# Masked softmax on one core: narrow loads into staging buffers, with a copy on VectorE

## The chip, the core and the metric

The kernel runs on one core of a Trainium2 chip. The metric is device time in microseconds, from one execution of the program. Before the change three runs gave 156.01, 156.16 and 156.28 us, median 156.16.

A core has engines that each follow an instruction queue of their own: VectorE (DVE in the profile), ScalarE (ACT), GpSimd (POOL), TensorE (PE) and SyncE (SP), which here only issues transfers. Sixteen DMA engines move data between HBM (the large memory, where inputs and outputs lie) and SBUF (the on-chip memory, 128 partitions wide). Engines wait for one another and for transfers by semaphores: counters that an instruction or a landed transfer raises and that another waits for.

## What is computed

The input `x` has 16 batches of 8 heads of 256 x 256 float32; `lengths` has one number per batch, between 128 and 255. Each row of 256 is softmaxed over its first `length` columns, and the other columns of the result are zero:

```python
for b in range(batch):
    length = lengths[b]
    masked = x[b, :, :, :length].copy()
    masked = masked - np.max(masked, axis=-1, keepdims=True)
    exp_masked = np.exp(masked)
    result[b, :, :, :length] = exp_masked / np.sum(exp_masked, axis=-1, keepdims=True)
```

The lengths of this draw are 188, 233, 229, 243 for the first four batches and 195, 252, 165, 210, 222, 180, 209, 157, 159, 199, 214, 248 for the other twelve.

## The kernel before

**Tiling.** A batch is 2,048 rows of 256 floats. It is one tile: 128 partitions with 16 rows (`nt`) of 1 KB each, 2.1 MB. A partition's 16 rows are neighbours in HBM. `xt` holds eight such tiles (`slots`), and batch b uses slot b % 8. Everything is done in place: loaded, masked, exponentiated, divided and stored from the same slot.

**Loads.** SP loads batches 0 to 3 whole, at the start (lines 128 to 132, batch 0 as two halves). The other twelve are issued by POOL in a loop (line 177). For each, POOL reads the batch's length into a register (line 180, the load itself is line 120) and walks a binary tree of branches, `pick`, that ends at one of twelve loads: the smallest of the widths 160, 168, ..., 240, 256 that is no less than the length. Only so many columns of each row are fetched, into a tile whose rows keep their distance of 1 KB (line 151). Widths here are 200, 256, 168, 216, 224, 184, 216, 160, 160, 200, 216, 256. From the third of these loads on, POOL first waits for the load two before it (`s_sw`, line 182) and, from batch 8 on, for the store of the batch eight before it, whose slot it takes (`s_st`, line 183; the semaphore starts with 64 counted, so that the first pair passes). Columns that a narrow load leaves out hold zeros from a fill (line 173) or what an earlier batch left there; the mask covers both.

**VectorE.** For each batch: `mask` (line 230) reads the length into a register, waits for the load, and in one instruction, `clip` (line 221), takes the minimum of x and a huge falling ramp `down` + `len_s`, which leaves the first `length` columns and makes the others hugely negative. Only the columns from 128 on are treated, since no length here is under 128; that is 128 x 2048 elements. `clip` raises `s_min` by two. After ScalarE's exponentials, `divide` (line 242) is done for each half of the rows: a reciprocal of the row sums (line 245) and a multiply (line 248).

The order on VectorE is fixed. For batch 0 and from batch 4 on it is divide(b, first half), mask(b+1), divide(b, second half); for batches 1 to 3 it is mask(b+1), divide(b, first half), divide(b, second half). So the mask of batch 4 stands ahead of both divides of batch 3.

**ScalarE** loops over 32 half tiles (line 321): it waits for `s_min`, then does eight exponentials of 256 elements with row sums (line 326). The slot is found in registers, as the loop's counter modulo 16.

**Stores.** SP issues one to three transfers per batch (`parts`, line 51; line 141), each when `divide` has raised `s_out`, and before the first of a batch it waits for the stores of the batch two before it (line 140). At the end SP waits for the last two batches' stores.

No maximum is subtracted. After the last batch VectorE tests that all row sums are within bounds, and an exact second pass stands ready if they aren't (from line 272); it isn't entered with this input.

Of the kernel before, what the change touches and what calls it, by code (L numbers as in the profile page):

```python
# [9 lines left out]
F32 = mybir.dt.float32  # L10
# [7 lines left out]
POOL = mybir.EngineType.Pool  # L18
# [3 lines left out]
def kernel(  # L22
# [6 lines left out]
    nc = tc.nc  # L29
    P = nc.NUM_PARTITIONS  # L30

    batch, heads, seq_q, seq_k = x.shape
    rows = heads * seq_q
    assert rows % P == 0
    nt = rows // P
# [3 lines left out]
    x_f = x.rearrange("b h q k -> b (h q) k").rearrange("b (p t) k -> b p t k", p=P)  # L39
    out_f = out.rearrange("b h q k -> b (h q) k").rearrange("b (p t) k -> b p t k", p=P)  # L40

    slots = 8
    ahead = 4
    assert slots - ahead == 4 and batch % slots == 0

    widths = list(range(160, 248, 8))
    low = widths[0]
    mid = seq_k // 2
# [15 lines left out]
    pool = ctx.enter_context(tc.tile_pool(name="all", bufs=1))  # L64
    psum = ctx.enter_context(tc.tile_pool(name="psum", bufs=1, space=bass.MemoryType.PSUM))
    xt = pool.tile([P, slots, nt, seq_k], F32, name="xt")
    word64 = pool.tile([1, batch], mybir.dt.int64, name="word64")
    word = word64.bitcast(I32)
    len_b = pool.tile([1, batch], BF16, name="len_b")
# [21 lines left out]
    sem = lambda n: ctx.enter_context(nc.semaphore(n))  # L91
    s_st = [sem("s_st0"), sem("s_st1")]
    with tc.tile_critical(no_gpsimd_drain=True):  # L93
# [3 lines left out]
        s_lenf = sem("s_lenf")  # L97
        s_ld = [sem(f"s_ld{k}") for k in range(ahead + 1)]

        s_sw = [sem("s_sw0"), sem("s_sw1")]  # L100

        s_iota = sem("s_iota")
        s_fill = sem("s_fill")
        s_v = sem("s_v")
        s_min = sem("s_min")
# [12 lines left out]
        def length(engine, at):  # L118

            return nc.values_load(  # L120
                at,
                engines=[engine],
                skip_runtime_bounds_check_because="compared with constants, never an address",
            )
# [3 lines left out]
        for h in range(2):  # L128
            s = slice(h * half, (h + 1) * half)
# [5 lines left out]
        for b in range(batch):  # L135
            s_b = s_st[b % 2]
            for s in parts(b):
                nc.sync.wait_ge(s_out, 2 * b + (s.stop - 1) // half + 1)
                if b >= 2 and s.start == 0:
                    nc.sync.wait_ge(s_b, 64 * (b // 2 + 1))  # L140
                nc.sync.dma_start(
                    out=out_f[b, :, s, :], in_=xt[:, b % slots, s, :]
# [1 line left out]

        def pick(v, n, slot, par, ws):

            if len(ws) == 1:
                w = ws[0]  # L150
                nc.gpsimd.dma_start(  # L151
                    out=xt[:, slot, :, :w], in_=x_n[:, n, :, :w]
                ).then_inc(s_sw[par], 16)
                return
            m = (len(ws) - 1) // 2
            with nc.gpsimd.If(v <= ws[m]):  # L156
                pick(v, n, slot, par, ws[: m + 1])
            with nc.gpsimd.Else():
                pick(v, n, slot, par, ws[m + 1 :])

        x_n = x_f.rearrange("b p t c -> p b t c")
        x_g = x_f.rearrange("b p t c -> p b (t c)")
# [6 lines left out]
        for par in range(2):  # L169
            nc.gpsimd.memset(seed[:, par : par + 1], 0.0).then_inc(s_st[par], 64)  # L170
        nc.gpsimd.wait_ge(s_v, 2)
        for b in range(ahead, slots):
            nc.gpsimd.memset(xt[:, b, :, low:], 0.0).then_inc(s_fill, 1)  # L173
        nc.gpsimd.wait_ge(s_word, 16)
        nc.gpsimd.wait_ge(s_fill, slots - ahead)
        nc.gpsimd.wait_ge(s_ld[ahead - 1], 16)
        with nc.Fori(0, (batch - ahead) // 2, 1, engines=[POOL]) as q:
            for par in range(2):
                n = 2 * q + (ahead + par)
                v_len = length(POOL, word[0:1, bass.ds(2 * n, 1)])  # L180
                with nc.gpsimd.If(q >= 1):  # L181
                    nc.gpsimd.wait_ge(s_sw[par], 16 * q)
                    nc.gpsimd.wait_ge(s_st[par], 64 * q)
                pick(v_len, bass.ds(n, 1), bass.ds(n % slots, 1), par, widths + [seq_k])


        nc.tensor.wait_ge(s_ones, 2)
# [6 lines left out]
        v = 0  # L194

        def step(ins):
# [8 lines left out]
                out=down, in0=iota_i, scalar1=0.5, scalar2=-big, op0=ALU.add, op1=ALU.mult  # L205
# [7 lines left out]
                out=len_s, in0=len_f, scalar1=big, scalar2=None, op0=ALU.mult  # L213
# [1 line left out]
        )  # L215
        nc.vector.wait_ge(s_v, v)

        def clip(b, s, lo, hi):

            t = xt[:, b % slots, s, lo:hi]  # L220
            return nc.vector.scalar_tensor_tensor(  # L221
                out=t,
                in0=down[:, None, lo:hi].to_broadcast([P, s.stop - s.start, hi - lo]),
                scalar=len_s[:, b : b + 1],
                in1=t,
                op0=ALU.add,
                op1=ALU.min,
            )

        def mask(b, s):  # L230
            v_len = length(DVE, word[0:1, 2 * b : 2 * b + 1])
            if b == 0:
                nc.vector.wait_ge(s_ld[s.start // half], 16)
            elif b < ahead:
                nc.vector.wait_ge(s_ld[b + 1], 16)
            else:
                nc.vector.wait_ge(s_sw[b % 2], 16 * ((b - ahead) // 2 + 1))
            with nc.vector.If(v_len < mid):
                clip(b, s, 0, mid)
            clip(b, s, mid, seq_k).then_inc(s_min, (s.stop - s.start) // half)  # L240

        def divide(b, h):
            s = slice(h * half, (h + 1) * half)
            nc.vector.wait_ge(s_exp, 2 * b + h + 1)
            step(nc.vector.reciprocal(out=inv_sum[:, b, s], in_=row_sum[:, b, s]))  # L245
            nc.vector.wait_ge(s_v, v)
            t = xt[:, b % slots, s, :]
            nc.vector.tensor_tensor(  # L248
                out=t,
                in0=t,  # L250
                in1=inv_sum[:, b, s, None].to_broadcast([P, half, seq_k]),
                op=ALU.mult,
            ).then_inc(s_out, 1)

        mask(0, slice(0, half))
        mask(0, slice(half, nt))
        for b in range(batch):


            first = b == 0 or b >= ahead  # L260
            if first:
                divide(b, 0)
            if b + 1 < batch:
                mask(b + 1, slice(0, nt))
            if not first:
                divide(b, 0)
            divide(b, 1)
# [8 lines left out]
        for k, (edge, op) in enumerate(((sum_high, ALU.is_gt), (sum_low, ALU.is_lt))):  # L276
            nc.vector.tensor_scalar(  # L277
                out=bad[:, k : k + 1],
# [13 lines left out]
        with nc.vector.Else():  # L292
            with nc.Fori(0, batch, 1, engines=[DVE]) as i:
                nc.vector.wait_ge(g_ld, 16 * i + 16)
                nc.vector.scalar_tensor_tensor(
                    out=g_t,
                    in0=down[:, None, :].to_broadcast([P, nt, seq_k]),
                    scalar=len_s[:, bass.ds(i, 1)],
                    in1=g_t,
# [5 lines left out]
                    out=neg_max, in_=g_t, op=ALU.max, axis=AX, negate=True  # L305
# [5 lines left out]
                    out=g_t,  # L311
                    in0=g_t,
                    in1=inv_g[:, :, None].to_broadcast([P, nt, seq_k]),
# [7 lines left out]
        with nc.Fori(0, 2 * batch, 1, engines=[ACT]) as i:  # L321
            nc.scalar.wait_ge(s_min, i + 1)
            at = bass.ds(i % (2 * slots), 1)
            for j in range(half):
                e = x_h[:, at, j, :]
                ins = nc.scalar.activation(  # L326
                    out=e, in_=e, func=EXP, accum_out=sum_h[:, bass.ds(i, 1), j]
# [5 lines left out]
        with nc.scalar.If(a_redo >= 1):  # L333
            for par in range(2):
                nc.scalar.wait_ge(s_st[par], 64 * (batch // 2 + 1))
            with nc.Fori(0, batch, 1, engines=[ACT]) as i:
                nc.scalar.dma_start(out=g_t, in_=x_g[:, bass.ds(i, 1)]).then_inc(g_ld, 16)
                nc.scalar.wait_ge(g_v, 3 * i + 2)
                for t in range(nt):
                    ins = nc.scalar.activation(  # L340
                        out=g_t[:, t],
                        in_=g_t[:, t],
# [43 lines left out]
```

## Time and profile before

| | before |
|---|---|
| median of three runs | 156.16 us |
| the profiled execution | 156.34 us |
| its span, first to last instruction | 154.7 us |
| DMA | 62.09 MB, 401 GB/s over the span |
| VectorE busy | 116.6 us (75%) |
| ScalarE busy | 105.2 us (68%) |
| POOL busy | 19.0 us (12%) |
| last multiply ends | 147.11 us |

The span lies inside the execution; the rest of 156.34 is outside what the instructions cover. A row of the profile names the source line (L221), the engine, the operation, the tiles (written <- read) and their shapes; behind a bar stand the busy time in us and the mean of one in ns, then the engine's idle time ahead of these instructions and what ended it. Engine names with a q, as POOLq, are the engine's instruction queue: register work, branches and the issuing of transfers. In the slice rows the span is cut into 40 equal parts, and a digit is the busy share in tenths. A queue row of the DMA part gives packets, MB, and the packets' time as a share of 16 engines' span; q1 carries SP's transfers, q0 those of POOL.

### The profile page before, as it was taken

The numbers are of one execution on the slowest core, as the hardware profiler recorded it, in microseconds if no ns is written. First come the engines' busy times: TensorE is split into PE (matmuls) and PEld (weight loads), VectorE is DVE, ScalarE is ACT, GpSimd is POOL, SyncE is SP. The second block draws the span as 40 slices with busy tenths as digits, with TensorE's granted clock in tenths as the row PEclk, the third lists the DMA queues.
The fourth block names the chain that finished last, engine by engine and source line by source line (L and its number), as shares of the span: only waits on it lengthen the run. The fifth ranks groups of instructions, "written<-read, shape, count | busy, mean of one in ns | idle before, by whom it ended". The sixth has DMA issues, their size and how long they took to land.

```text
span 154.7 us, 1341 instructions
## 1 busy us (share of the span) xinstructions
PE 0.3 (0%) x2; PEld 0.2 (0%) x2; DVE 116.6 (75%) x89; ACT 105.2 (68%) x514; POOL 19.0 (12%) x26
## 2 busy tenths in 40 slices
PE   0000000000000000000000000000000000000000
PEld 0000000000000000000000000000000000000000
DVE  1349999953999696979879696969669619696820
ACT  3097799992692959688695959595964914959300
POOL 4910031000220200202020020202001000000000
DMA  3999999999999999999999999999999999999991
GB/s 114 430 447 419 441 373 420 403 407 447 406 403 391 410 410 417 412 416 412 404 422 409 415 412 409 421 414 412 415 424 415 416 437 432 422 447 424 424 426 76
DMA packets 9989, 62.09 MB, mean 401 GB/s; under 512 B 850, under 2 KB 946, under 8 KB 6274
## 3 DMA queue, kind: packets, MB, share of 16 engines
q1 hardware_dynamic: 5904, 41.95, 65.7%
q0 software_dynamic: 4080, 20.12, 32.1%
q14 instruction: 3, 0.02, 0.0%
q10 hardware_dynamic: 2, 0.00, 0.0%
HBM read 28.51 MB, written 33.55 MB: 401 GB/s over the span
## 4 chain that ended last, share of the span: by engine, by line
DMA 77%; issue 7%; DVE 4%; ACT 3%; POOLq 3%; SPq 1%; ACTq 0%; POOL 0%; PE 0%; DVEq 0%
DMA xt<-in_x_dram 77%; ACT xt L326 3%; DVE xt L221 2%; DVE xt L248 1%; POOLq L120 1%; POOLq L156 1%; POOLq L151 1%; SPq L130 1%; DVE ends L274 0%; ACTq L326 0%; POOL xt L151 0%; SPq L132 0%; POOLq L181 0%; DVE bad L277 0%; DVE inv_sum L245 0%
## 5 line engine op out<-in xcount | busy, mean ns | idle before, releaser
L326 ACT ACTIVATE xt<-xt x256 | 102.4, 402 | 37.7 <-DVE xt L221 37.7
L248 DVE TENSOR_TENSOR xt<-xt,inv_sum 128x2048 f32<-128x2048 f32 x32 | 73.3, 2291 | 1.1
L326 ACT ACTIVATION_READ_ACCUMULATOR xt<-xt x256 | 48.0, 188 | 0.0
L221 DVE SCALAR_TENSOR_TENSOR xt<-down,len_s,xt 128x2048 f32<-128x2048 f32 (+1 forms) x17 | 37.8, 2221 | 13.6 <-DMA xt<-in_x_dram 13.5
L151 POOL DMA_DIRECT2D xt<-in_x_dram x12 | 12.8, 1064 | 96.0 <-DMA out_dram<-xt 54.2
L245 DVE RECIPROCAL inv_sum<-row_sum 128x8 f32<-128x8 f32 x32 | 6.3, 198 | 14.4 <-ACT xt L326 14.4
L173 POOL MEMSET xt<- 128x1536 f32 x4 | 5.3, 1391 | 1.1 <-DVE len_s L212 1.1
L318 ACT ACT_TABLE_LOAD x1 | 1.3, 1283 | 1.6 <-SPq L93 1.6
L204 DVE TENSOR_SCALAR down<-iota_i 128x256 f32<-128x256 int32 x1 | 0.3, 301 | 1.6 <-POOL iota_i L164 1.6
L274 DVE TENSOR_REDUCE ends<-row_sum 128x1 f32<-128x256 f32 x2 | 0.7, 411 | 0.0
L191 PE MATMUL count<-bad,ones_c 128*1 128x2 bf16 x1 | 0.2, 164 | 145.3 <-DVE bad L277 145.3
L209 DVE CAST len_b<-word 1x16 bf16<-1x16 int32 x1 | 0.2, 164 | 0.4 <-DMA word<-in_lengths_dram 0.4
L212 DVE TENSOR_SCALAR len_s<-len_f 128x16 f32<-128x16 f32 x1 | 0.2, 173 | 0.3 <-PE len_f L189 0.3
L164 POOL IOTA iota_i<- 128x256 int32 x1 | 0.3, 331 | 0.6 <-SPq L93 0.6
L285 DVE TENSOR_REDUCE redo<-count 1x1 f32<-1x2 f32 x1 | 0.1, 148 | 0.3 <-PE count L191 0.3
L191 PEld LDWEIGHTS count<-bad,ones_c 128*1 128x1 bf16 x1 | 0.1, 79 | 145.4 <-DVE bad L277 145.4
L170 POOL MEMSET seed<- 1x1 f32 x2 | 0.2, 226 | 0.0
L277 DVE TENSOR_SCALAR bad<-ends 128x1 bf16<-128x1 f32 x2 | 0.2, 152 | 0.0
L318 ACT ACTIVATE warm<-const-float32-0.0 128x1 f32<-128x1 f32 x1 | 0.2, 204 | 0.0
L167 POOL MEMSET ones<- 1x128 bf16 x1 | 0.2, 196 | 0.0
L189 PE MATMUL len_f<-len_b,ones 1*128 1x16 bf16 x1 | 0.2, 165 | 2.6 <-DVE len_b L209 2.6
L370 POOL MEMSET const-float32-0.0<- 128x1 f32 x1 | 0.1, 98 | 0.3 <-issue 0.3
(6 smaller groups left out, 0.5 us busy)
## 6 DMA issues: line engine op xcount, KB each, us to landing
out_dram<-xt SPq DMA_DIRECT2D x19, 1024.0 KB
out_dram<-xt SPq DMA_DIRECT2D x14, 512.0 KB
xt<-in_x_dram SPq DMA_DIRECT2D x3, 2048.0 KB, 16.0
out_dram<-xt SPq DMA_DIRECT2D x3, 2048.0 KB
xt<-in_x_dram POOLq DMA_DIRECT2D x3, 1728.0 KB, 16.9
xt<-in_x_dram POOLq DMA_DIRECT2D x2, 2048.0 KB, 18.5
xt<-in_x_dram POOLq DMA_DIRECT2D x2, 1600.0 KB, 17.1
xt<-in_x_dram POOLq DMA_DIRECT2D x2, 1280.0 KB, 15.1
```

Of the source, the lines that this page charges most:

```text
L120: return nc.values_load(at, engines=[engine], skip_runtime_bounds_check_because="compared with constants, never an address",)
L130: nc.sync.dma_start(out=xt[:, 0, s], in_=x_f[0, :, s]).then_inc(s_ld[h], 16)
L151: nc.gpsimd.dma_start(out=xt[:, slot, :, :w], in_=x_n[:, n, :, :w]).then_inc(s_sw[par], 16)
L156: with nc.gpsimd.If(v <= ws[m]):
L173: nc.gpsimd.memset(xt[:, b, :, low:], 0.0).then_inc(s_fill, 1)
L191: nc.tensor.matmul(count, lhsT=ones_c, rhs=bad, start=True, stop=True).then_inc(s_count, 1)
L221: return nc.vector.scalar_tensor_tensor(out=t, in0=down[:, None, lo:hi].to_broadcast([P, s.stop - s.start, hi - lo]), scalar=len_s[:, b : ...
L245: step(nc.vector.reciprocal(out=inv_sum[:, b, s], in_=row_sum[:, b, s]))
L248: nc.vector.tensor_tensor(out=t, in0=t, in1=inv_sum[:, b, s, None].to_broadcast([P, half, seq_k]), op=ALU.mult,).then_inc(s_out, 1)
L274: step(nc.vector.tensor_reduce(out=ends[:, k : k + 1], in_=sums, op=op, axis=AX))
L318: nc.scalar.activation(out=warm, in_=nc.const_aps.tensor(0.0, (P, 1), F32), func=EXP)
L326: ins = nc.scalar.activation(out=e, in_=e, func=EXP, accum_out=sum_h[:, bass.ds(i, 1), j])
```

## The change

`xt` has six slots instead of eight, and four buffers `raw` of a tile's size are added. POOL's twelve loads go into `raw`, batch n into buffer (n - 4) % 4, with a partition's 16 rows of w columns lying one behind the other, without gaps. Each buffer has a semaphore of its own, `s_sw[k]`. POOL's loop now runs three times over four loads; from the fifth load on, a load waits until `s_min` shows that the batch four before it has been masked, and no longer for a load or a store.

On VectorE `mask` hands batches from 4 on to a new function, `spread`. It waits, from batch 6 on, for the store of the batch six before it (whose slot of `xt` it takes) and for its load. Then it walks the same binary tree over the widths, since the rows' distance in `raw` is known only by the width, and at the end of the tree copies columns 0 to 127 of the 16 rows into the tile and clips columns 128 to 255 out of `raw` into the tile. For the narrowest width a further branch chooses clip instead of copy for the left half where the length is under 128. The fill on POOL now covers the end of each `raw` buffer, and is as large as before. ScalarE's slot is the counter modulo 12. Stores, divides and the order on VectorE stay.

```diff
-    slots = 8
+    slots = 6
     ahead = 4
+    stages = 4
...
+    raw = pool.tile([P, stages, nt * seq_k], F32, name="raw")
...
-        def pick(v, n, slot, par, ws):
+        def pick(v, n, k, ws):
...
                 nc.gpsimd.dma_start(
-                    out=xt[:, slot, :, :w], in_=x_n[:, n, :, :w]
-                ).then_inc(s_sw[par], 16)
+                    out=raw[:, k, : nt * w], in_=x_n[:, n, :, :w]
+                ).then_inc(s_sw[k], 16)
...
-        for b in range(ahead, slots):
-            nc.gpsimd.memset(xt[:, b, :, low:], 0.0).then_inc(s_fill, 1)
+        for k in range(stages):
+            nc.gpsimd.memset(raw[:, k, nt * low :], 0.0).then_inc(s_fill, 1)
...
-        with nc.Fori(0, (batch - ahead) // 2, 1, engines=[POOL]) as q:
-            for par in range(2):
-                n = 2 * q + (ahead + par)
+        with nc.Fori(0, (batch - ahead) // stages, 1, engines=[POOL]) as q:
+            for k in range(stages):
+                n = stages * q + (ahead + k)
                 v_len = length(POOL, word[0:1, bass.ds(2 * n, 1)])
                 with nc.gpsimd.If(q >= 1):
-                    nc.gpsimd.wait_ge(s_sw[par], 16 * q)
-                    nc.gpsimd.wait_ge(s_st[par], 64 * q)
-                pick(v_len, bass.ds(n, 1), bass.ds(n % slots, 1), par, widths + [seq_k])
+                    nc.gpsimd.wait_ge(s_min, 2 * stages * q + 2 * (ahead + k - stages + 1))
+                pick(v_len, bass.ds(n, 1), k, widths + [seq_k])
...
-        def clip(b, s, lo, hi):
+        def clip(b, s, lo, hi, src=None):
...
-                in1=t,
+                in1=t if src is None else src,
...
-                nc.vector.wait_ge(s_sw[b % 2], 16 * ((b - ahead) // 2 + 1))
+                return spread(b, v_len)
...
+        def spread(b, v_len):
+            k = (b - ahead) % stages
+            if b >= slots:
+                nc.vector.wait_ge(s_st[b % 2], 64 * ((b - slots) // 2 + 2))
+            nc.vector.wait_ge(s_sw[k], 16 * ((b - ahead) // stages + 1))
+
+            def rows(w, lo, hi):
+                if w == seq_k:
+                    return raw[:, k].rearrange("p (t c) -> p t c", c=w)[:, :, lo:hi]
+                return raw[:, k, lo : lo + nt * w].rearrange("p (t c) -> p t c", c=w)[
+                    :, :, : hi - lo
+                ]
+
+            every = slice(0, nt)
+
+            def choose(ws):
+                if len(ws) > 1:
+                    m = (len(ws) - 1) // 2
+                    with nc.vector.If(v_len <= ws[m]):
+                        choose(ws[: m + 1])
+                    with nc.vector.Else():
+                        choose(ws[m + 1 :])
+                    return
+                w = ws[0]
+                left = rows(w, 0, mid)
+                if w == low:
+                    with nc.vector.If(v_len < mid):
+                        clip(b, every, 0, mid, left)
+                    with nc.vector.Else():
+                        nc.vector.tensor_copy(out=xt[:, b % slots, :, :mid], in_=left)
+                else:
+                    nc.vector.tensor_copy(out=xt[:, b % slots, :, :mid], in_=left)
+                clip(b, every, mid, seq_k, rows(w, mid, seq_k)).then_inc(s_min, 2)
+
+            choose(widths + [seq_k])
```

## The prediction

> **What bounds the kernel now.** I read the page's totals first, then the DMA part, then VectorE's timeline, since two things run close to the end together here.
>
> The page of before, its engine totals, its DMA slices and its queues:
>
> ```profile
> PE 0.3 (0%) x2; PEld 0.2 (0%) x2; DVE 116.6 (75%) x89; ACT 105.2 (68%) x514; POOL 19.0 (12%) x26
> DMA  3999999999999999999999999999999999999991
> DMA packets 9989, 62.09 MB, mean 401 GB/s; under 512 B 850, under 2 KB 946, under 8 KB 6274
> q1 hardware_dynamic: 5904, 41.95, 65.7%
> q0 software_dynamic: 4080, 20.12, 32.1%
> ```
>
> DMA is full from the first load to the last store. The two queues take 97.8% of 154.7 us, 151.3 us of all 16 engines. This is the bound today. VectorE, at 75%, looks free. Its timeline says how free (start, duration, instruction, and in brackets the idle time before it):
>
> ```profile
> 30.83 2.29 DVE L248 TENSOR_TENSOR xt<-xt,inv_sum 128x2048 f32<-128x2048 f32 x1
> 37.51 2.35 DVE L221 SCALAR_TENSOR_TENSOR xt<-down,len_s,xt 128x2048 f32<-128x2048 f32 x1 [4.39 <-DMA xt<-in_x_dram]
> ...
> 78.15 0.20 DVE L245 RECIPROCAL inv_sum<-row_sum 128x8 f32<-128x8 f32 x1 [1.15 <-ACT xt L326]
> 78.39 2.29 DVE L248 TENSOR_TENSOR xt<-xt,inv_sum 128x2048 f32<-128x2048 f32 x1
> 80.60 2.35 DVE L221 SCALAR_TENSOR_TENSOR xt<-down,len_s,xt 128x2048 f32<-128x2048 f32 x1
> 82.86 0.19 DVE L245 RECIPROCAL inv_sum<-row_sum 128x8 f32<-128x8 f32 x1
> 83.09 2.29 DVE L248 TENSOR_TENSOR xt<-xt,inv_sum 128x2048 f32<-128x2048 f32 x1
> 86.53 0.20 DVE L245 RECIPROCAL inv_sum<-row_sum 128x8 f32<-128x8 f32 x1 [1.15 <-ACT xt L326]
> ...
> 127.08 2.35 DVE L221 SCALAR_TENSOR_TENSOR xt<-down,len_s,xt 128x2048 f32<-128x2048 f32 x1 [3.25 <-DMA xt<-in_x_dram]
> 135.47 2.34 DVE L221 SCALAR_TENSOR_TENSOR xt<-down,len_s,xt 128x2048 f32<-128x2048 f32 x1
> 144.82 2.29 DVE L248 TENSOR_TENSOR xt<-xt,inv_sum 128x2048 f32<-128x2048 f32 x1
> ```
>
> Clips (L221) of the middle tiles start every 8.38 us, whatever the width loaded. That is a closed ring: clip (2.26 from start to next start), ScalarE's first eight exponentials (the reciprocal starts 3.67 after the clip ends), reciprocal and multiply (2.45). Inside it VectorE idles only 1.15 us. So the compute is not DMA's guest with room to spare. It is a second bound, about 9 us behind: DMA waits inserted 4.39 us before the clip of batch 4, and between the clips of 4 and 15 the distance is 97.96 where a ring never kept waiting takes 9.58 + 10 x 8.38 = 93.4 (the first period, 9.58, holds one multiply more), another 4.6. Together 9.0 us.
>
> **The change part by part.** The profiled execution took 156.34 us with a span of 154.7; the median shown is 156.16. I sum against the span and add the difference to the median.
>
> Loads four ahead. A load now waits for VectorE's clip of four batches earlier, no longer for a store. POOL's wait rows show what goes:
>
> ```profile
> POOL xt L151 <- DMA out_dram<-xt: 54.2, 7, 9.1
> ```
>
> Loads of batches 4 to 7 issue one after the other from 20.8 us (some 3.2 us apart, as the first two are today), and later ones with four rings of lead. The waits behind the 4.6 us then go: -4.6. The 4.39 depends on when load 4 lands. Its 1.64 MB took from 20.77 to 37.3, because its packets (records in the trace of 4,320 to 4,800 bytes, five to seven rows) alternate with store and load packets of 16,384 and then 8,192 and 4,096. Packet against packet at 0.41 MB/us (402 GB/s in that stretch) I get 35.4: 0.76 MB while 2.5 MB in 16 KB packets leave (0.4 left of load 3, and store 0), the rest against the smaller ones of store 1, plus 1.3 to land. Measured is 37.3, so the picture holds to 1.9 us. A row group whose 16 rows lie one behind the other in the buffer is one piece of 10 to 14 KB. If it travels as one packet, load 4 gets 12.8/(12.8+16) = 44%, 9.1 us, landing at 31.2, or 33.1 with the same error. VectorE is free at 33.1 (30.83 + 2.29). Taken: -4.4, ends 0 and -4.4.
>
> The Trainium skill, DMA: Bandwidth & Descriptors, SWDGE vs HWDGE vs iDMA, says that a packet is preferably at most 4,096 B. The narrow records above agree, the 16,384 B records of whole tiles do not. By that rule nothing of the 4.4 would come, and the time would be that of the first rival below.
>
> Copy. Twelve copies of 128x2048 f32, one in each ring before its clip, nothing beside them since the clip and ScalarE wait behind. No f32 copy is in the trace. The nearest one-input row is L204, 128x256 in 301 ns; against fixed costs of 164 (L209, 16 elements) to 198 ns (L245) that is 0.42 to 0.57 ns an element, so 1.05 to 1.32 us for 2048, less 0.08 which neighbours overlap (2.35 lasts, 2.26 to the next start). The far end is the two-input clip, 2.35. I take 1.2, by L204: +14.4, ends +11.6 and +27.
>
> Choosing on VectorE. Each batch walks a tree of three or four branches. POOL's same tree (L181 to the last L156 in the chain, 43.47 to 44.09) costs 0.6. VectorE's register load before it takes 0.31 to 1.53 (L120, median 0.75) and its branch 0.06. All of it issues while the preceding multiply runs for 2.29, so 0; if the cover is gone, up to 0.6 a batch. Behind the new wait for the store of six batches earlier stand the clip, the multiply after it and ScalarE. At 9.6 us a ring against 1.68 + 2.10 MB a tile (9.2 us at 0.41) that store, five rings old, is done: 0. Should stores lag, DMA is full again and the wait only moves.
>
> ScalarE's slot index is now taken modulo 12 instead of 16, in register operations ahead of each half. One is 0.035 to 0.105 long (L326). Zero to three more, exposed once a ring: +0.5, ends 0 and +2.
>
> Fills on POOL (four of 1.39) stay the same size and end before 9 us, beside the initial loads: 0. Store issues and their waits on SP are the same instructions. POOL's register work for the slot falls away, off the path.
>
> Packets. From the records, 4,096 B take 0.162 us and 16,384 B 0.611, which leaves 12 ns fixed per packet. Ten narrow loads in row groups save some 147 packets an engine: 1.8 us of DMA time if merged, 0 if not. DMA no longer sets the end, so 0 in the sum.
>
> Tail. The last multiply ends at 147.11, the last store is confirmed at 153.5 since DMA is behind: 6.4. With DMA ahead only the last 1 MB stores remain: issue 0.4, 2.4 at 428 GB/s (136 to 148), a little of the half before it, 1.3 to land, 4.4 in all. -2.0, ends -3.4 and 0.
>
> Sum: -4.6 - 4.4 + 14.4 + 0.5 - 2.0 = +3.9. Span 158.6, time 156.16 + 3.9 = 160.1.
>
> **The rivals.**
> Loads still land late: narrow loads go on in packets of about 4 KB, load 4 lands at 37.3 as today and the 4.39 stays. For it: every narrow record is just over 4,096 B. Against: whole tiles travel in pieces as long as the destination's. 160.1 + 4.4 = 164.5.
>
> Faster: the copy is cheap. Place: VectorE's ring. With c for the copy the sum is -10.5 + 12c, so below 0.88 us the ring is no longer last. DMA then is, with 1.8 us less work: about 154.4. For it: the ring's 9.0 us of waiting. Against: even L245's higher fixed cost leaves 0.97.
>
> The copy runs like a two-input instruction, 2.26 net: 12 x 1.06 more, 172.8. For it only that the other large rows on VectorE all run at 1.1 ns an element; against it L204.
>
> The tree is exposed by half a microsecond a batch: 160.1 + 6 = 166. The register load's longest, 1.53, and the tree's 0.6 come within 0.2 of the multiply's 2.29.
>
> Jumps stall VectorE's queue. Straight code of a few instructions a batch becomes trees of an estimated 50, of which most are jumped over. If a jump has to wait for instructions as long as a register load's round trip (1.53 at most), about 1 us of it shows past the multiply; three such stalls give 163, one in each batch 172. Against it: the same tree on POOL shows no step over 0.16 us. The Trainium skill, Runtime: NRT & Kernel Launch, Instruction fetch mechanics, says that a taken branch out of a window of two blocks of 256 instructions waits for a fetch. By that rule some 600 new instructions have two or three places for it; no run here shows one.
>
> **How the numbers follow.** Forecast 46% (157.3 to 163: copy 0.97 to 1.25, index 0 to 2, half a microsecond of tail). Late loads 32% (161.5 to 167). Copy at full price 6%. Tree exposed 4%, jumps 2% (163). Faster 7%. A copy near 0.88, within 0.2%, 3%; 0.2% is about what a measurement of this kernel can tell from no change. Slower is thus 46 + 32 + 6 + 4 + 2 = 90%. From 157 to 167 holds the first two cases with the tree's and the jumps', and leaves out the dear copy and the faster case.
>
> **What would show it.** VectorE's timeline: copies of about 1.2 us, clips 9.6 us apart, no DMA wait before the clip of batch 4 and none at 127. DMA slices below 9 in the last third. POOL's wait row for stores gone; the tail after the last multiply some 4 us. Packet sizes: merged if the count of q0 falls from 4,080 to about 1,700. Wrong would be: copies outside 1.0 to 1.3, gaps between multiply and copy, waits of VectorE for stores, or DMA still full to the end.

## The result, and the profile after

The changed kernel takes 164.51 us in the median of its runs (164.42 to 164.63), against 156.22 for the kernel before on the same chip: 1.0533 times as long, with an interval of 1.0515 to 1.0552. The forecast of 160.1 had the sign and the engine that sets the end, but only 3.9 of the 8.3 us. The time lies in the range, at the value of the first rival, "Loads still land late".

The profiled execution took 164.63 us, with a span of 163.0. The page of after, in the same parts as for before (engine totals, DMA slices, queues, shares of the chain, the group of the copies):

```profile
PE 0.3 (0%) x2; PEld 0.2 (0%) x2; DVE 130.1 (80%) x101; ACT 105.2 (65%) x514; POOL 19.0 (12%) x26
DMA  4999999999999999999999999999999997390995
DMA packets 9995, 62.14 MB, mean 381 GB/s; under 512 B 850, under 2 KB 946, under 8 KB 6274
q0 software_dynamic: 4080, 20.12, 30.7%
DVE 35%; DMA 23%; issue 18%; ACT 14%; ACTq 4%; DVEq 2%; SPq 1%; POOLq 1%; PE 0%
L276 DVE COPY xt<-raw 128x2048 f32<-128x2048 f32 x10 | 12.2, 1220 | 5.4 <-DMA raw<-in_x_dram 5.4
```

Three things are to be seen. DMA is no longer full at the end, and the chain that ended last runs through VectorE (35%) and no longer through DMA (77% before). A copy takes 1.22 us, as forecast. And POOL's queue, q0, still moves its 20.12 MB in 4,080 packets: rows that lie one behind the other in the buffer were not merged.

How far DMA has fallen back shows in one late stretch, 136 to 148 us. The columns are length, busy time (and instructions) of PE, PEld, DVE, ACT and POOL, the TensorE clock, DMA's busy share and its GB/s. Before:

```profile
136.00:148.00 12.00, 0.00 (x0) 0.00 (x0) 10.06 (x11) 6.67 (x34) 0.00 (x0) 1.00 1.00 428
```

After:

```profile
136.00:148.00 12.00, 0.00 (x0) 0.00 (x0) 10.79 (x9) 6.49 (x32) 0.00 (x0) 1.00 0.54 230
```

VectorE's timeline of after:

```profile
30.92 2.29 DVE L287 TENSOR_TENSOR xt<-xt,inv_sum 128x2048 f32<-128x2048 f32 x1
38.58 1.23 DVE L276 COPY xt<-raw 128x2048 f32<-128x2048 f32 x1 [5.37 <-DMA raw<-in_x_dram]
39.73 2.35 DVE L222 SCALAR_TENSOR_TENSOR xt<-down,len_s,raw 128x2048 f32<-128x2048 f32 x1
...
85.14 2.29 DVE L287 TENSOR_TENSOR xt<-xt,inv_sum 128x2048 f32<-128x2048 f32 x1
87.35 1.22 DVE L276 COPY xt<-raw 128x2048 f32<-128x2048 f32 x1
88.48 2.34 DVE L222 SCALAR_TENSOR_TENSOR xt<-down,len_s,raw 128x2048 f32<-128x2048 f32 x1
...
96.86 1.22 DVE L276 COPY xt<-raw 128x2048 f32<-128x2048 f32 x1
...
145.54 2.35 DVE L222 SCALAR_TENSOR_TENSOR xt<-down,len_s,raw 128x2048 f32<-128x2048 f32 x1
154.90 2.29 DVE L287 TENSOR_TENSOR xt<-xt,inv_sum 128x2048 f32<-128x2048 f32 x1
```

A ring is now 96.86 - 87.35 = 9.51 us; it was 8.375, so a copy adds 1.135. The copy starts when the multiply before it is done (85.14 + 2.29 = 87.43, with the usual overlap of 0.08): nothing of the tree's branches shows between them. From the clip of batch 4 to that of batch 15 it is 145.54 - 39.73 = 105.81. A ring that is never kept waiting takes 9.58 + 1.135 + 10 x 9.51 = 105.8. So behind batch 4 there is no wait left on this chain, neither for a load nor for a store.

But the wait before batch 4 is still there. It was 4.39 us and is 5.37, and VectorE's first instruction on the batch starts at 38.58 instead of 37.51.

The sum, measured in the two profiles, against the one forecast:

| | forecast | measured | from |
|---|---|---|---|
| waits in the middle | -4.6 | -4.6 | clips 4 to 15, above |
| wait before batch 4 | -4.4 | +1.07 | 37.51 to 38.58 |
| twelve copies | +14.4 | +13.6 | 12 x 1.135 |
| index modulo 12 | +0.5 | 0 | ring 9.51 = 8.375 + 1.135 |
| tail | -2.0 | -1.8 | 6.4 to 4.6 (161.8 - 157.2) |
| sum | +3.9 | +8.3 | span 154.7 to 163.0 |

### The profile page after: what moved, and what is told of

Read it like the earlier page. It is cut to its first block, busy times and chain, and to the rows that moved or that the text cites. A ratio compares the mean times of both kernels' runs of the same rounds, so it can differ in the third digit from the quotient of the medians.

```text
span 163.0 us, 1389 instructions
## 1 busy us (share of the span) xinstructions
PE 0.3 (0%) x2; PEld 0.2 (0%) x2; DVE 130.1 (80%) x101; ACT 105.2 (65%) x514; POOL 19.0 (12%) x26
## 3 DMA queue, kind: packets, MB, share of 16 engines
q0 software_dynamic: 4080, 20.12, 30.7%
## 4 chain that ended last, share of the span: by engine, by line
DVE 35%; DMA 23%; issue 18%; ACT 14%; ACTq 4%; DVEq 2%; SPq 1%; POOLq 1%; PE 0%
DVE xt L222 17%; ACT xt L365 14%; DMA raw<-in_x_dram 11%; DMA xt<-in_x_dram 10%; DVE xt L287 8%; DVE xt L276 7%; ACTq L365 3%; DMA out_dram<-xt 2%; DVE inv_sum L284 2%; DVE xt L274 1%; DVEq L263 1%; SPq L132 0%; DVE ends L313 0%; POOLq L122 0%; ACTq L360 0%
## 5 line engine op out<-in xcount | busy, mean ns | idle before, releaser
L222 DVE SCALAR_TENSOR_TENSOR xt<-down,len_s,raw 128x2048 f32<-128x2048 f32 x12 | 28.1, 2344 | 0.0
L153 POOL DMA_DIRECT2D raw<-in_x_dram x12 | 12.8, 1063 | 90.6 <-issue 90.6
L284 DVE RECIPROCAL inv_sum<-row_sum 128x8 f32<-128x8 f32 x32 | 6.3, 198 | 14.4 <-ACT xt L365 14.4
L276 DVE COPY xt<-raw 128x2048 f32<-128x2048 f32 x10 | 12.2, 1220 | 5.4 <-DMA raw<-in_x_dram 5.4
L222 DVE SCALAR_TENSOR_TENSOR xt<-down,len_s,xt 128x2048 f32<-128x2048 f32 (+1 forms) x5 | 9.6, 1924 | 4.9 <-DMA xt<-in_x_dram 4.8
L175 POOL MEMSET raw<- 128x1536 f32 x4 | 5.3, 1391 | 1.1 <-DVE len_s L213 1.1
L274 DVE COPY xt<-raw 128x2048 f32<-128x2048 f32 x2 | 2.4, 1218 | 0.0
## 6 DMA issues: line engine op xcount, KB each, us to landing
raw<-in_x_dram POOLq DMA_DIRECT2D x2, 1600.0 KB, 20.3
```

The source lines that it names most:

```text
L153: nc.gpsimd.dma_start(out=raw[:, k, : nt * w], in_=x_n[:, n, :, :w]).then_inc(s_sw[k], 16)
L175: nc.gpsimd.memset(raw[:, k, nt * low :], 0.0).then_inc(s_fill, 1)
L222: return nc.vector.scalar_tensor_tensor(out=t, in0=down[:, None, lo:hi].to_broadcast([P, s.stop - s.start, hi - lo]), scalar=len_s[:, b : ...
L274: nc.vector.tensor_copy(out=xt[:, b % slots, :, :mid], in_=left)
L276: nc.vector.tensor_copy(out=xt[:, b % slots, :, :mid], in_=left)
```

## The experiments

Except where an edit says "before", it is made in the changed kernel. Ratios are against the kernel before, run on the same chip; on each of the chips its median lies between 156.05 and 156.22 us, so the medians can be compared with one another too.

| run | median, us | ratio (95%) |
|---|---|---|
| e1, no copies | 158.85 | 1.0177 (1.0157 to 1.0196) |
| e2, copies twice | 180.01 | 1.1531 (1.1508 to 1.1554) |
| e3, store 0 in quarters | 162.50 | 1.0413 (1.0395 to 1.0430) |
| e4, batch 4 whole | 160.50 | 1.0285 (1.0267 to 1.0304) |
| e5, store 0 in quarters, before | 156.66 | 1.0036 (1.0023 to 1.0050) |
| e6, eight slots | 164.51 | 1.0538 (1.0519 to 1.0557) |
| e7, two staging buffers | 167.95 | 1.0737 (1.0708 to 1.0766) |
| e8, POOL copies | 159.63 | 1.0215 (1.0194 to 1.0236) |
| e9, first load earlier | 163.71 | 1.0482 (1.0453 to 1.0510) |
| e10, tree alone, before | 159.16 | 1.0188 (1.0165 to 1.0211) |
| e11, halves stored, before | 160.03 | 1.0243 (1.0215 to 1.0271) |
| e12, no copies, eight slots | 159.28 | 1.0202 (1.0175 to 1.0228) |
| e13, no tree | 163.89 | 1.0498 (1.0479 to 1.0517) |
| e14, tree for six batches, before | 157.40 | 1.0075 (1.0062 to 1.0088) |

### The copy

**e1** leaves the copies out (and zeroes columns 0 to 127 of slots 4 and 5 once, so that the left halves hold numbers).

```diff
-                else:
-                    nc.vector.tensor_copy(out=xt[:, b % slots, :, :mid], in_=left)
```

> The changed kernel without the copy of columns 0 to 127 for batches 4 to 15, so those columns of the result are not this input's; waits, tree, staging and six tiles stay. Ring theory (the copy lengthens VectorE's ring of 9.51 us, and that ring sets the end): the ring is 8.38 again, the last multiply ends at 157.2 - 12 x 1.13 = 143.6, earlier than in the kernel before, and DMA with its 151 us of work is last again: 156.3 (155.8 to 157). Rival (six tiles and the waits for stores, or loads four ahead that hold up the stores, cost the time): 164 or within 1 us of it.

**e2** makes each copy twice, the second waiting for the first.

```diff
+                    nc.vector.tensor_copy(out=xt[:, b % slots, :, :mid], in_=left).then_inc(s_v, 1)
+                    nc.vector.wait_ge(s_v, v + 1)
                     nc.vector.tensor_copy(out=xt[:, b % slots, :, :mid], in_=left)
```

> The changed kernel with every copy done twice, the second after a wait for the first. Ring theory: 12 times 1.13 to 1.3 us more, 178.1 to 180. Rival (stores or loads set the end, VectorE has slack): at most 167.

e2 costs 15.5 us more than the changed kernel, 1.29 for each of twelve. VectorE's timeline of e2 has the pair, 1.26 apart:

```profile
82.97 1.22 DVE L279 COPY xt<-raw 128x2048 f32<-128x2048 f32 x1
84.23 1.23 DVE L281 COPY xt<-raw 128x2048 f32<-128x2048 f32 x1
```

So each copy lies on the path at its whole price, and none of it is hidden. Taking them away gives back only 5.7 us, since without them the ring is 8.38 again and DMA is last. The DMA slices of e1 and its timeline before batch 14:

```profile
DMA  4999999999999999999999999999999999999970
...
127.33 2.35 DVE L224 SCALAR_TENSOR_TENSOR xt<-down,len_s,raw 128x2048 f32<-128x2048 f32 x1 [3.87 <-DMA out_dram<-xt]
```

All sixteen DMA engines are busy until 152.1 us, and the 3.87 us is once more a wait for DMA. The profile puts it down to a store, but the store of batch 8, whose slot batch 14 takes, had landed by 111.2 us, while the last part of load 14 lands at 126.67, just ahead of the clip. It is a wait for the load. That a DMA-bound kernel is back was expected; that it takes 158.85 and not 156.3 was not. The section on the tree takes this up.

### The first narrow load

Why does batch 4 still land late? Theory: its narrow packets share the DMA engines, packet by packet, with larger ones, the 16,384 B packets of the initial whole loads and of store 0 above all. Rival: it is the bytes queued ahead that count.

**e4** loads batch 4 alone whole (with POOL's loop written out), which is 28% more bytes but in large packets.

```diff
-                pick(v_len, bass.ds(n, 1), k, widths + [seq_k])
+                pick(v_len, slice(n, n + 1), (n - ahead) % stages, [seq_k] if n == ahead else widths + [seq_k])
...
-            choose(widths + [seq_k])
+            choose([seq_k] if b == ahead else widths + [seq_k])
```

> The changed kernel with batch 4 loaded at the full width of 256 columns, 28% more bytes, in packets of 16,384 B; POOL's loop is written out, the other loads are as they were. Packet theory: half of DMA instead of 23%, landing at 32 to 34, the end 4.5 to 5.5 us earlier: 159.5 (159 to 160.5). Rival (bytes and queue order): 0.46 MB more, landing at 40 or later, 166 to 167.

VectorE's timeline of e4, the copy of batch 4:

```profile
34.11 1.23 DVE L274 COPY xt<-raw 128x2048 f32<-128x2048 f32 x1 [1.18 <-DMA raw<-in_x_dram]
```

More bytes arrive 4.5 us earlier, and the time falls by 4.0 us, from 164.51 to 160.50. The rival falls. The packets are not the only difference, though: in e4 the load's first packet also moves earlier, at 22.4 us instead of 26.5, which e9 below takes up. In the records of after, while load 4 competes with 8,192 B store packets (29 to 32 us), each of the two queues starts 95 packets, of 4,800 and 8,192 B, which makes 0.152 and 0.259 MB/us. In e4, from 24 to 32 us, it is 102 packets against 105, all of 16,384 B, and both move 0.21. So a queue's share goes by the size of its packets, one against one.

**e3** cuts the store of batch 0 into quarters, which makes its packets 4,096 B.

```diff
-            cuts = [0, nt]
+            cuts = [0, quarter, half, half + quarter, nt]
```

> The changed kernel with the store of batch 0 issued in four quarters, whose packets are 4,096 B instead of 16,384 B. Packet theory (load 4 lands late because its packets of 4,800 B alternate with packets of 16,384 B): it gets over half of DMA once load 3 is through, lands at 30.5 to 32.5 instead of 38.1, VectorE does not wait for it, and the end comes 5.2 us earlier: 159.2 (158.7 to 160). Rival (load 4 is late for its bytes, or because three more loads stand behind it): 164.5.

VectorE's timeline of e3:

```profile
36.14 1.23 DVE L276 COPY xt<-raw 128x2048 f32<-128x2048 f32 x1 [3.08 <-DMA raw<-in_x_dram]
```

The direction is right, but the gain is 2.0 us and not 5.3. The records say why: POOL issues load 4 at 20.8 us in the changed kernel, but its first packet only moves at 26.5, and in e3 almost two thirds of the store are through by then (332 of 512 packets). Between issue and first packet lie 5.8 us in which POOL's queue has nothing else to move; for the whole load of e4 it is 3.4 (19.0 to 22.4). The picture behind the prediction, in which the load moves from 20.8, was wrong.

**e9** asks whether this late start is what costs: POOL waits for batch 1 instead of batch 2 before it issues.

```diff
-nc.gpsimd.wait_ge(s_ld[ahead - 1], 16)
+nc.gpsimd.wait_ge(s_ld[ahead - 2], 16)
```

> The changed kernel in which POOL issues load 4 when batch 1 has landed (13.7 us) instead of batch 2 (18.5). In the changed kernel load 4's first packet moved 5.7 us after POOL's instruction though its queue was empty. Start theory (that delay, as well as the shares of the queue, makes load 4 late): the first packet goes at about 21.5, load 4 lands some 4 us earlier, the end comes 3.5 to 5 us earlier: 160.2 (159.5 to 161.2). If the shares alone count, since until 26 only 16 KB packets stand against it: 1 us earlier at most, 163.5 to 164.5.

VectorE's timeline of e9:

```profile
37.55 1.23 DVE L276 COPY xt<-raw 128x2048 f32<-128x2048 f32 x1 [4.23 <-DMA raw<-in_x_dram]
```

The first packet now moves at 20.3, 6 us earlier, and batch 4 is there 1.0 us earlier. Until 31 us the load starts 213 packets of 4,800 B beside 182 of 16,384 B, which makes 0.10 MB/us against 0.28. The share is what costs; the start is worth little by itself.

**e5** makes the cut of e3 in the kernel before.

> The kernel before with the store of batch 0 in four quarters. Packet theory: load 4 lands by 32 here too, so VectorE's wait of 4.39 us goes; but DMA sets the end of this kernel, so the time stays: 156.2 (155.9 to 156.7). Rival (a wait removed from VectorE's chain is worth its length in this kernel too): 151.8.

VectorE's timeline of e5 before batch 4, and SP's last wait:

```profile
35.74 2.35 DVE L221 SCALAR_TENSOR_TENSOR xt<-down,len_s,xt 128x2048 f32<-128x2048 f32 x1 [2.56 <-DMA xt<-in_x_dram]
...
SPq L381 <- DMA out_dram<-xt: 7.2, 1, 7.2
```

Batch 4 is 1.8 us earlier (not 4.39, since here too the load starts late), VectorE ends 3.8 us earlier (143.2 against 147.0 for its last reduction), and the kernel is 0.6 us slower: there DMA ends last, and SP waits for it 7.2 us. A wait before batch 4 is worth something only where VectorE's ring sets the end. After the change it does.

### The slots and the four loads in flight

**e6** gives the tiles eight slots again, so that VectorE's new wait for a store can't bind.

```diff
-    slots = 6
+    slots = 8
```

> The changed kernel with eight tiles instead of six beside the four staging buffers. Ring theory: no wait of VectorE is for a store, so nothing changes: 164.5 (164.2 to 164.8). It also drops the division by 12 for the slot, which by the ring's 9.51 = 8.375 + 1.135 costs nothing. Rival (six tiles hold up VectorE or the stores): 160 or less.

No difference, and the ring is 87.09 - 77.57 = 9.52 in VectorE's timeline of e6:

```profile
77.57 1.22 DVE L276 COPY xt<-raw 128x2048 f32<-128x2048 f32 x1
...
87.09 1.22 DVE L276 COPY xt<-raw 128x2048 f32<-128x2048 f32 x1
```

Six slots cost nothing, nor does the modulo of 12.

**e7** has two staging buffers instead of four.

```diff
-    stages = 4
+    stages = 2
```

> The changed kernel with two staging buffers and two loads in flight. Ring theory: a load then has some 15 us from its issue to its copy, and loads with at most one ahead took 13 to 18 us in the kernel before; a few waits of VectorE of 1 to 2 us, 164.5 to 167. Rival (loads four ahead starve the stores, which costs the time): 162 or less. If four in flight is worth much: over 168.

VectorE's timeline of e7, two of its waits:

```profile
70.15 1.23 DVE L276 COPY xt<-raw 128x2048 f32<-128x2048 f32 x1 [2.40 <-DMA out_dram<-xt]
...
128.39 1.23 DVE L276 COPY xt<-raw 128x2048 f32<-128x2048 f32 x1 [1.06 <-DMA raw<-in_x_dram]
```

It is 3.4 us slower than with four, 1 us more than the ring theory's upper end. The profile puts the first of the two waits down to a store, but the store of batch 1, whose slot batch 7 takes, had landed by 45 us, and the last part of load 7 lands at 69.48: both are waits for loads. So the four loads in flight do what they are there for, given the staging: they remove waits. The rival, that loads far ahead starve the stores, falls.

### The copy on another engine

**e8** lets POOL copy and VectorE only clip. POOL then walks the tree twice a batch.

```diff
+                nc.gpsimd.tensor_copy(
+                    out=xt[:, at, :, :mid],
+                    in_=raw[:, k, : nt * w].rearrange("p (t c) -> p t c", c=w)[:, :, :mid],
+                ).then_inc(s_cp, 1)
...
+            nc.vector.wait_ge(s_cp, b - ahead + 1)
```

> The changed kernel with the copies on POOL, which waits for the load and the store in VectorE's place and copies while VectorE is still at the batch before; VectorE clips only. Ring theory: VectorE's ring is 8.38 again, DMA is last: 156.2 to 157.5, if a copy on POOL takes under 4 us (its fills ran at 0.9 ns an element, so some 2 us). Rival (tiles, stores, loads ahead): 164. If POOL and VectorE hinder each other: multiplies or clips over 2.35 us and a time in between.

Groups and timeline of e8 (in the groups, behind the count: shortest/median/longest in ns, first and last start):

```profile
L183 POOL COPY xt<-raw x12: 1891/2050/3202, 37.7 to 134.9; 128x2048 f32<-128x2048 f32 x12
L300 DVE TENSOR_TENSOR xt<-xt,inv_sum x32: 2291/2293/3749, 11.6 to 149.0; 128x2048 f32<-128x2048 f32 x32
...
40.08 2.35 DVE L245 SCALAR_TENSOR_TENSOR xt<-down,len_s,raw 128x2048 f32<-128x2048 f32 x1 [7.01 <-POOL xt L183]
...
45.02 3.75 DVE L300 TENSOR_TENSOR xt<-xt,inv_sum 128x2048 f32<-128x2048 f32 x1
```

4.9 us better than the changed kernel, and still 2% behind the one before. The copies are off VectorE, but VectorE waits 7.01 us for the first of them, and a multiply that has a POOL copy beside it (44.64 to 46.63) takes 3.75 instead of 2.29 us; nine others take 2.50. The Trainium skill, SBUF — State Buffer, Who interferes with whom, says that VectorE and GpSimd share a pair of ports under an exclusive lock. The 3.75 agrees; the copy beside it took 1.99, against 1.89 for the first copy, beside an idle VectorE, so here it was the multiply that was held up.

### The tree on VectorE

e1 left 2.8 us over the kernel before, without a copy. Candidates were the six slots and the tree of branches that VectorE walks per batch.

**e12** is e1 with eight slots.

```diff
-    slots = 6
+    slots = 8
```

> Changed kernel without copies, as in the run without copies (158.85), with eight tiles instead of six; columns 0 to 127 of batches 4 to 15 again are not this input's. That run waited 3.9 us for a store and ended 2.6 us after the kernel before although its ring was 8.38. If six tiles cost those 2.6 us: 156 to 156.8. If DMA sets the end in both, and one engine's extra transfers (instructions) are the 2.6 us: 158.5 to 159.2.

It takes 159.28, no better: the slots are not it. VectorE's wait in the same place of e12:

```profile
127.62 2.35 DVE L224 SCALAR_TENSOR_TENSOR xt<-down,len_s,raw 128x2048 f32<-128x2048 f32 x1 [4.01 <-DMA out_dram<-xt]
```

Here batch 14 takes the slot of batch 6, whose store had landed by 93 us, and the last part of load 14 lands at 126.96. So in e1 and e12 alike VectorE waited for the load, and not for a store, as was supposed ahead of e12.

**e10** adds nothing but the tree to the kernel before. At each of its ends stands the same clip (at the narrowest, as in the change, behind one branch more).

```diff
-            clip(b, s, mid, seq_k).then_inc(s_min, (s.stop - s.start) // half)
+            if b >= ahead:
+                choose(widths + [seq_k])
+            else:
+                clip(b, s, mid, seq_k).then_inc(s_min, (s.stop - s.start) // half)
```

> The kernel before, with the tree over the widths added on VectorE for batches 4 to 15, the same clip in place at each of its ends: more instructions to fetch, the same work. Fetch theory (instructions come as 8 KB transfers over the same DMA engines, six more of them in the changed kernel, about 0.3 us each on one engine, and show where DMA sets the end): instruction packets rise from 3 to some 8, 157.5 to 158.5. Rival (the fetches and the tree are hidden): 156.05 to 156.4.

The tree alone costs 3.0 us (156.12 to 159.16), more than the 1.4 to 2.4 of the fetch theory. The queue of instruction transfers in the kernel before:

```profile
q14 instruction: 3, 0.02, 0.0%
```

The same queue and VectorE's timeline in e10:

```profile
q14 instruction: 7, 0.06, 0.1%
...
128.44 2.35 DVE L221 SCALAR_TENSOR_TENSOR xt<-down,len_s,xt 128x2048 f32<-128x2048 f32 x1 [4.01 <-DMA xt<-in_x_dram]
```

The last data packet ends at 156.0 instead of 153.0 us; VectorE's last reduction is only 1.4 us later. So it is DMA that ends later, on the same data. But it isn't full until then. Half of the sixteen engines have work until 152.7 us, 1.1 us later than before. From 153.2 to 156.0 only one packet at a time is in flight, nine of 8,192 B in a row; in the kernel before that last stretch is 0.4 us long.

**e14** keeps the tree for batches 4 to 9 only.

```diff
-            if b >= ahead:
+            if ahead <= b < ahead + 6:
```

> The kernel before with the tree on VectorE for batches 4 to 9 alone instead of 4 to 15. If the 3.0 us of the full tree grow with the instructions: 1.2 to 1.8 us, 157.3 to 158. If they come from the late batches, when one wait lengthens the chain: under 0.5. If they are fixed: 3.

It costs 1.2 us (157.40), with 5 packets in q14 where before has 3 and e10 has 7, and the last data packet ends at 154.2, with 1.0 us of one packet at a time ahead of it. The cost grows with the amount of code.

**e13** asks what the tree costs in the changed kernel, where DMA isn't last: VectorE reads every buffer as if it were 256 wide, without a tree.

```diff
-            choose(widths + [seq_k])
+            choose([seq_k])
```

> The changed kernel without VectorE's tree: it reads every staging buffer as if its rows were 256 wide, so the result of narrow batches is not the reference's; all loads, copies and clips keep their number and size. If the tree is hidden behind the multiplies and shows only once, behind the wait for load 4: 0.3 us less, 164.0 to 164.3. If it adds to VectorE's chain or to DMA as it did in the kernel before: 161 to 162.

It is 0.6 us faster (164.51 to 163.89; in the two profiles 1.1, with a span of 161.9). In the profiles all of it lies before batch 4, whose copy starts 1.17 us earlier than in the changed kernel; VectorE's timeline of e13:

```profile
37.41 1.23 DVE L276 COPY xt<-raw 128x2048 f32<-128x2048 f32 x1 [4.17 <-DMA raw<-in_x_dram]
```

The landings in the traces divide the +1.07 of the sum. A load raises its semaphore in sixteen parts, as its parts land. Fifteen parts of load 4 are there at 36.83 us, before and after the change; the last comes at 37.27 before and at 38.07 after. From there to VectorE's first instruction it takes 0.24 us before, 0.51 after, with the tree's branches, and 0.02 in e13, where the last part lands at 37.39. So 0.27 of the 1.07 is the tree, which lies in the open once, where VectorE waits, and 0.80 is one late part. In other runs with the tree the last part of load 4 lands between 37.18 (e8) and 37.97 us (e12), so that this part is the tree's doing is not shown.

Later in the kernel such a part shows what the tree does. How long the sixteenth part of a load lands behind the fifteenth, in us:

| | load 4 | load 8 | load 11 | load 14 | load 15 |
|---|---|---|---|---|---|
| before | 0.44 | 0.41 | 0.38 | 0.27 | 0.29 |
| e13, no tree | 0.48 | 0.21 | 0.19 | 0.21 | 0.20 |
| after | 1.24 | 0.28 | 1.02 | 2.32 | 3.25 |
| e1, no copies | 1.01 | 0.89 | 1.69 | 2.91 | 2.87 |
| e10, tree alone, before | 0.49 | 0.15 | 1.19 | 1.03 | 1.03 |

In the two kernels without the tree it stays under 0.6 us for all twelve loads. With the tree it grows, in e1 by 0.8 to 1.0 us after each of the instruction transfers at 67.3, 93.1 and 118.4 us, and VectorE waits for the last part. The one packet at a time at the end of e10 fits this: it looks like fifteen engines that are through and one that still has work, though the records don't name the engine. After the change nothing behind batch 4 waits on VectorE's chain, and the late parts there cost nothing. Why an instruction transfer, which takes 0.31 us, sets a part back by about 1 us stays open.

**e11** tried another cost of DMA in the kernel before: batches 1 to 7 stored in two pieces instead of three, for fewer and larger packets.

```diff
-            cuts = [0, half, half + quarter, nt]
+            cuts = [0, half, nt]
```

> The kernel before with batches 1 to 7 stored in two halves instead of a half and two quarters: 896 packets fewer, at 12 ns fixed each 0.67 us less on each engine. Packet-cost theory: 155.4 (155.1 to 155.7). Rival (larger store packets hold up the narrow loads, VectorE waits longer and the last tile is late): 156.3 to 158.

It is 3.9 us slower with 1,008 packets fewer. VectorE's timeline of e11 and the window from 136 to 148 us:

```profile
79.50 2.35 DVE L221 SCALAR_TENSOR_TENSOR xt<-down,len_s,xt 128x2048 f32<-128x2048 f32 x1 [3.37 <-DMA xt<-in_x_dram]
...
136.00:148.00 12.00, 0.00 (x0) 0.00 (x0) 9.60 (x8) 10.12 (x52) 0.00 (x0) 1.00 0.69 290
```

Waits for loads now stand at 38.6 (5.42), at 67.7 (2.64) and here, with smaller ones later, and DMA has idle time late (0.69), where it had none. That fits the shares above: larger store packets take more of the engines from the narrow loads, and VectorE waits.

## Why the prediction was right or wrong

**What bounds the kernel: right.** VectorE's ring stood 9 us behind DMA, and a copy in the ring turned the order round. e5 shows the one side (VectorE 3.8 us earlier, nothing gained), e2 the other (twelve more copies, 15.5 us more).

**The copy: right, 0.065 too large each.** 1.135 from start to start against 1.2, well inside 0.97 to 1.25. The cheap copy (the faster rival) and the copy at a two-input price are both out.

**Loads four ahead, the 4.6 in the middle: right.** Nothing is left of it, and POOL's row for waits on stores is gone; after the change its loads have only this one ("issue" is time in which the engine waited for nothing that the profile shows):

```profile
POOL raw L153 <- issue: 90.6, 12, 12.4
```

**Loads four ahead, the wait before batch 4: wrong, and this is the step that failed.** "If it travels as one packet ... Taken: -4.4". It doesn't: 4,080 packets as before, and the records have the same 4,320 to 4,800 B. I took the piece's length in the buffer for the packet's, with no narrow load into a dense buffer in the trace. There was one clue for it, that whole tiles travel in pieces as long as the destination's, and one against, that every narrow record ends just past 4,096 B. The clue against was the one from the same kind of load. By the Trainium skill, DMA: Bandwidth & Descriptors, SWDGE vs HWDGE vs iDMA, a packet is preferably at most 4,096 B, and nothing of the 4.4 would come; the unchanged 4,080 agrees. What happened in its place: the load got 0.15 MB/us beside store packets of 8,192 B, it started 5.8 us after its issue, which my picture left out, and the wait grew from 4.39 to 5.37 us. Whether one packet per piece would have taken the whole 4.4 no run shows: e4, with packets of 16,384 B and 28% more bytes, still waits 1.18 before batch 4.

**Choosing on VectorE: 0 was mis-sized.** In the ring it is 0, as said: the copy follows the multiply without a gap. "Tree exposed" and "jumps" are out as prices per batch. But where VectorE waits for load 4 the tree's branches lie in the open once, 0.51 us instead of 0.24; without the tree the median is 0.6 lower (e13). And the tree costs 3.0 where DMA is last (e10), by one late part of sixteen, which the prediction had no term for. By the Trainium skill, Runtime: NRT & Kernel Launch, Instruction fetch mechanics, a taken branch out of the window waits for a fetch. In the ring no such stall shows: the 105.81 us between clips 4 and 15 leave no room for one.

**Index, slots, the wait for a store: 0** where I had +0.5 (e6).

**Tail: right,** -1.8 for -2.0.

**The first rival gave 164.5, the measured time.** Its mechanism, load 4 as late as before, is the one that happened. That the number agrees to 0.1 is partly luck: the copy (-0.8) and the index (-0.5) came out cheaper, the wait before batch 4 (+1.07) and the tail (+0.2) dearer. Its chance of 32% against 46% was too low for the evidence there was: the chances hung on one unknown, and the nearer row spoke for the rival.

What the change does with its parts apart: the staging without the copy (158.85) takes about what the kernel before takes with the tree (159.16). More loads in flight gain nothing where DMA is last anyway, and the copy then makes VectorE last. None of these versions beats the kernel before.

## What to carry to other kernels

Before an instruction is added to an engine with 25% idle time, find the ring it stands in: what counts is the time from one start to the next if nothing waits (8.38 us here), and how far that ring is behind the bound (9 us); twelve times 1.135 is more, and no gain in the loads brings that back. A load's share of busy DMA engines goes by the size of its packets against those it meets, so read the packets' sizes in the records, and don't infer them from the layout at the destination. And remove a wait only where the chain that ends last passes through it: the same cut gained 2.0 us after the change (e3) and lost 0.6 before it (e5). Where a wait can be for two things, compare the landings: in e1, e7 and e12 the label named a store, and it was the load.

## What the runs showed of the hardware that was not expected

- Narrow loads issued by POOL go in packets of 4,320 to 4,800 B (and a smaller rest of each piece), whether the rows land 1 KB apart or one behind the other in a piece of up to 14 KB: 4,080 packets for 20.12 MB both times.
- From POOL's instruction to the first packet of a narrow load 4.5 (e9) to 5.8 us (after) passed with nothing else in its queue; for a whole tile it was 3.4 us (e4).
- Two busy queues share the engines packet for packet, as the prediction assumed: 95 packets each in 3 us, so 0.152 and 0.259 MB/us for 4,800 and 8,192 B, and 0.21 each for 16,384 B. Fewer, larger store packets made the kernel slower by 2.4% (e11).
- A tree of branches on VectorE that adds no work cost 3.0 us in the DMA-bound kernel, and 1.2 us at half its size (e10, e14). One of the sixteen parts of the loads falls behind the others, up to 3.25 us (after), and in e1 by steps after transfers of instructions. Why such a transfer costs more than its 0.31 us is open.
- A POOL copy of 128 x 2048 takes 1.89 to 3.20 us, against 1.22 on VectorE, and can stretch a VectorE multiply from 2.29 to 3.75 us.
